# Rolling an 8192 x 8192 matrix by 100 columns: long pieces from column 100 on, and only the wrapped columns through SBUF

## The chip, the cores and the metric

The kernel runs on one core of a Trainium2 chip. The metric is the time of one execution on the device, in microseconds (us). Before the change the median of three runs was 828.28 us (827.91 to 828.41). The core has several engines that issue work: SP and ACT, which here only issue transfers; POOL, which issues transfers through a queue of its own; and DVE, which copies inside SBUF, the core's on-chip memory of 128 partitions. All transfers, whoever issued them, are carried out by 16 DMA engines.

## The reference

```python
def setup_inputs():
    return {"x": np.random.randn(8192, 8192).astype(np.float32), "shift": 100}

def reference(x, shift):
    return np.roll(x, shift, axis=1)
```

Every row is moved 100 columns to the right, and its last 100 columns come round to its beginning: `out[r, 100:] = x[r, :8092]` and `out[r, :100] = x[r, 8092:]`. Nothing is computed; 268.44 MB are read and 268.44 MB are written.

## The kernel before

Each output row is split at a column `a`. With a shift `s = 100`, L20 rounds it up to 128, and L21 and L22 add another 128, so `a = 256`. `g = a - s = 156` is the number of columns between the wrapped part and the split.

**The long pieces** (L36 to L43) are columns 256 to 8191 of the output. They are copied from memory to memory without passing SBUF. A block is 64 rows; the view takes its rows as 16 x 4, and for each of the four values of `j` one transfer moves 16 rows of 7936 columns (31,744 bytes a row, 496 KB a transfer). SP issues those of even `j`, ACT those of odd `j`. There are 128 blocks. In the last four, each transfer is cut into two halves at a column `mid`, so that the last transfers are smaller. SP and ACT thus issue 264 transfers each. In bytes of a row, a long piece is read from byte 624 (column 156) and written from byte 1024 (column 256).

**The edge pieces** (L60 to L80) are columns 0 to 255 of the output. They go through SBUF in 16 stages of 512 rows, four consecutive rows on each of 128 partitions. A stage has a tile `h` that collects the 256 columns of its 512 rows, and a tile `t`.

- L72 loads `t`. In memory the end of a row is followed by the beginning of the next one, so one run of 256 columns holds the last 100 columns of a row and the first 156 of the next row. Each partition loads three such runs, of 1024 bytes.
- L73 loads the last 100 columns of the fourth row (400 bytes) straight into `h`, and L76 the first 156 columns of the first row (624 bytes).
- L74 and L77 are copies on DVE that bring the two parts of the three runs to their places in `h`.
- L80, in a loop of its own after all stages, stores `h`: 512 runs of 1024 bytes, 512 KB, at byte 0 of the output rows.

All loads and stores of the edge pieces are issued by POOL, in the order of the program: three loads for each of 16 stages and then 16 stores. The tiles of all stages fit beside one another (`bufs=n_st`), so no stage waits for a buffer of another. POOL does wait when too many of its transfers are under way, and a store waits for the copies of its stage. The output columns of the two kinds of pieces don't overlap, so neither waits for the other.

Of the kernel before, what the change touches and what calls it, by code (L numbers as in the profile page):

```python
# [1 line left out]

# [4 lines left out]


@with_exitstack
def kernel(  # L10
    ctx: ExitStack,
    tc: tile.TileContext,
    x: bass.AP,
    shift: int,
    out: bass.AP,
):
    nc = tc.nc
    n_rows, n_cols = x.shape
    s = shift % n_cols
    a = -(-s // 128) * 128  # L20
    if 0 < a <= 384 and a + 128 <= n_cols:  # L21
        a += 128  # L22
    g = a - s
    P = nc.NUM_PARTITIONS
    engines = [nc.sync, nc.scalar]
    n_chunks = 16
    rows = n_rows // n_chunks

    xm = x.rearrange("(c e j) w -> c j e w", e=16, j=4)
    om = out.rearrange("(c e j) w -> c j e w", e=16, j=4)
    if a < n_cols:  # L36
        blocks = n_rows // 64
        mid = (a + n_cols) // 256 * 128
        for c in range(blocks):
            parts = ((a, mid), (mid, n_cols)) if c >= blocks - 4 and a < mid else ((a, n_cols),)  # L40
            for j in range(4):
                for lo, hi in parts:
                    engines[j % 2].dma_start(out=om[c, j, :, lo:hi], in_=xm[c, j, :, lo - s:hi - s])  # L43
    if a == 0:
        return


    if a > 512:
        for i in range(n_chunks):
            r = slice(i * rows, (i + 1) * rows)  # L50
            nc.gpsimd.dma_start(out=out[r, :s], in_=x[r, n_cols - s:])
            if g > 0:
                nc.gpsimd.dma_start(out=out[r, s:a], in_=x[r, :g])
        return

    Q = 4  # L60
    n_st = n_rows // (P * Q)
    reads = ctx.enter_context(tc.tile_pool(name="reads", bufs=n_st))
    heads = ctx.enter_context(tc.tile_pool(name="heads", bufs=n_st))
    xt = x.rearrange("(k p q) c -> k p q c", q=Q, p=P)
    ot = out.rearrange("(k p q) c -> k p q c", q=Q, p=P)
    tiles = []
    for k in range(n_st):
        t = reads.tile([P, Q - 1, a], x.dtype)
        h = heads.tile([P, Q, a], x.dtype)
        lead = bass.AP(tensor=x.tensor, offset=(k * P * Q + 1) * n_cols - s,  # L70
                       ap=[[Q * n_cols, P], [n_cols, Q - 1], [1, a]])
        nc.gpsimd.dma_start(out=t[:], in_=lead)  # L72
        nc.gpsimd.dma_start(out=h[:, Q - 1, :s], in_=xt[k, :, Q - 1, n_cols - s:])  # L73
        nc.vector.tensor_copy(h[:, :Q - 1, :s], t[:, :, :s])  # L74
        if g > 0:
            nc.gpsimd.dma_start(out=h[:, 0, s:], in_=xt[k, :, 0, :g])  # L76
            nc.vector.tensor_copy(h[:, 1:, s:], t[:, :, s:])  # L77
        tiles.append(h)
    for k, h in enumerate(tiles):
        nc.gpsimd.dma_start(out=ot[k, :, :, :a], in_=h[:])  # L80


# [1 line left out]
_INS = ['x', 'shift']  # L84
_OUTS = [((8192, 8192), 'float32')]

_NUMBERS = {'shift': 100}


# [26 lines left out]
```

## Time and profile before

| | |
|---|---|
| Median of three runs | 828.28 us (827.91 to 828.41) |
| Span of the profiled execution | 828.0 us |
| Long pieces, SP's and ACT's queues | 2 x 130.04 MB |
| Edge pieces, POOL's queue | 16.78 MB |
| Mean rate of the DMA engines | 334 GB/s |
| Memory traffic, read and written | 648 GB/s |
| Busy: DVE, POOL | 12.3 us, 41.3 us |
| Landing of a long transfer after its issue, median | 12.7 us |
| Landing of an edge store after its issue, median | 108.2 us |

The profiled execution is known by its span alone, from the first to the last instruction, 828.0 us, which is 0.3 us from the median of the runs. The profile's rate of the DMA engines counts a moved byte once. Its memory traffic counts a byte of a long piece twice, since it is read from memory and written to memory, and a byte of an edge piece once in its load and once in its store, since the other end of each is in SBUF. Queue rows give packets, megabytes and the share of the 16 engines' time that the packets took; an engine is occupied while it waits for memory too. In the views of the profile, q1 and q10 are the queues of SP and ACT, q0 is POOL's.

### The profile page before, as it was taken

The page shows a single profiled execution, that of the slowest core. Times are in us where ns is not written, and L with a number is a line of the kernel's source. Part 1 is how long each engine was busy: PE and PEld are TensorE (multiplying, and loading weights), DVE is VectorE, ACT ScalarE, POOL GpSimd, SP SyncE. Part 2 cuts the span into 40 slices and gives each one's busy share as a digit, 9 for nine tenths or more (in the row PEclk, how much of TensorE's full clock was granted, in tenths as well). Part 3 has the DMA queues.
Part 4 walks back from the last instruction along what each step waited for, and adds up shares of the span by engine and source line. Part 5 has one row for each costly group of instructions (what it writes and reads, how often), then busy time and mean ns, then how long its engine had stood idle before and what let it go on. Part 6 is the DMA issues. An engine that isn't in the chain of part 4 may idle for free. (4 is left out here: it accounts for less than half of the span.)

```text
span 828.0 us, 689 instructions
## 1 busy us (share of the span) xinstructions
DVE 12.3 (1%) x32; POOL 41.3 (5%) x68
## 2 busy tenths in 40 slices
DVE  0000000000010000000000000000000000000000
POOL 2011000000021100000000000000000000000000
DMA  9999999999999999999999999999999999999998
GB/s 308 340 350 334 344 340 337 337 339 344 337 342 348 352 351 345 354 339 346 347 341 344 333 325 325 319 330 333 330 324 322 335 330 328 322 331 328 327 314 300
DMA packets 22278, 276.90 MB, mean 334 GB/s; under 512 B 9473, under 2 KB 9729, under 8 KB 13825
## 3 DMA queue, kind: packets, MB, share of 16 engines
q1 hardware_dynamic: 8448, 130.04, 46.1%
q10 hardware_dynamic: 8448, 130.04, 44.7%
q0 software_dynamic: 5376, 16.78, 8.4%
q14 instruction: 6, 0.04, 0.0%
HBM read 268.44 MB, written 268.44 MB: 648 GB/s over the span
## 5 line engine op out<-in xcount | busy, mean ns | idle before, releaser
L80 POOL DMA_DIRECT2D out_dram<-h x16 | 11.5, 724 | 126.6 <-DMA out_dram<-h 86.8
L76 POOL DMA_DIRECT2D h<-in_x_dram x16 | 8.7, 542 | 141.4 <-DMA t<-in_x_dram 141.4
L72 POOL DMA_DIRECT2D t<-in_x_dram x16 | 12.2, 762 | 30.8 <-DMA h<-in_x_dram 30.0
L73 POOL DMA_DIRECT2D h<-in_x_dram x16 | 8.9, 559 | 39.9 <-DMA h<-in_x_dram 39.9
L74 DVE COPY h<-t 128x300 f32<-128x300 f32 x16 | 6.1, 382 | 260.2 <-DMA t<-in_x_dram 260.2
L77 DVE COPY h<-t 128x468 f32<-128x468 f32 x16 | 7.5, 467 | 0.0
L97 POOL MEMSET const-float32-0.0<- 128x1 f32 x1 | 0.1, 99 | 0.2 <-issue 0.2
L97 POOL MEMSET const-bfloat16-1.0<- 128x1 bf16 x1 | 0.1, 102 | 0.0
L97 POOL MEMSET const-float32-1.0<- 128x1 f32 x1 | 0.1, 99 | 0.0
L97 POOL MEMSET const-uint8-127<- 128x1 uint8 x1 | 0.1, 99 | 0.0
## 6 DMA issues: line engine op xcount, KB each, us to landing
out_dram<-in_x_dram ACTq DMA_DIRECT2D x248, 496.0 KB, 12.7
out_dram<-in_x_dram SPq DMA_DIRECT2D x248, 496.0 KB, 12.7
out_dram<-h POOLq DMA_DIRECT2D x16, 512.0 KB, 108.2
t<-in_x_dram POOLq DMA_DIRECT2D x16, 384.0 KB, 50.6
out_dram<-in_x_dram SPq DMA_DIRECT2D x16, 248.0 KB, 6.0
out_dram<-in_x_dram ACTq DMA_DIRECT2D x16, 248.0 KB, 5.9
h<-in_x_dram POOLq DMA_DIRECT2D x16, 78.0 KB, 43.2
h<-in_x_dram POOLq DMA_DIRECT2D x16, 50.0 KB, 49.9
```

What stands on the lines that cost most here:

```text
L72: nc.gpsimd.dma_start(out=t[:], in_=lead)
L73: nc.gpsimd.dma_start(out=h[:, Q - 1, :s], in_=xt[k, :, Q - 1, n_cols - s:])
L74: nc.vector.tensor_copy(h[:, :Q - 1, :s], t[:, :, :s])
L76: nc.gpsimd.dma_start(out=h[:, 0, s:], in_=xt[k, :, 0, :g])
L77: nc.vector.tensor_copy(h[:, 1:, s:], t[:, :, s:])
L80: nc.gpsimd.dma_start(out=ot[k, :, :, :a], in_=h[:])
L97: nc = _bacc.Bacc("TRN2", target_bir_lowering=False, num_devices=1)
```

## The change

`a` becomes the shift itself, 100, so `g` is 0. The long pieces are now columns 100 to 8191: 8092 columns, 32,368 bytes a row, read from byte 0 of a row and written from byte 400. `mid` becomes 4096, so the halves in the last four blocks have 3996 and 4096 columns instead of 3968 each. Of the edge pieces only the 100 wrapped columns are left. A stage has one tile, one load of 512 runs of 400 bytes and one store of the same runs at byte 0 of the output rows. The tile `t`, the loads of L72, L73 and L76 and the copies on DVE are gone.

```diff
     s = shift % n_cols
-    a = -(-s // 128) * 128
-    if 0 < a <= 384 and a + 128 <= n_cols:
-        a += 128
+    a = s
     g = a - s
...
     Q = 4
     n_st = n_rows // (P * Q)
-    reads = ctx.enter_context(tc.tile_pool(name="reads", bufs=n_st))
-    heads = ctx.enter_context(tc.tile_pool(name="heads", bufs=n_st))
+    ends = ctx.enter_context(tc.tile_pool(name="ends", bufs=n_st))
...
     for k in range(n_st):
-        t = reads.tile([P, Q - 1, a], x.dtype)
-        h = heads.tile([P, Q, a], x.dtype)
-        lead = bass.AP(tensor=x.tensor, offset=(k * P * Q + 1) * n_cols - s,
-                       ap=[[Q * n_cols, P], [n_cols, Q - 1], [1, a]])
-        nc.gpsimd.dma_start(out=t[:], in_=lead)
-        nc.gpsimd.dma_start(out=h[:, Q - 1, :s], in_=xt[k, :, Q - 1, n_cols - s:])
-        nc.vector.tensor_copy(h[:, :Q - 1, :s], t[:, :, :s])
-        if g > 0:
-            nc.gpsimd.dma_start(out=h[:, 0, s:], in_=xt[k, :, 0, :g])
-            nc.vector.tensor_copy(h[:, 1:, s:], t[:, :, s:])
+        h = ends.tile([P, Q, s], x.dtype)
+        nc.gpsimd.dma_start(out=h[:], in_=xt[k, :, :, n_cols - s:])
         tiles.append(h)
     for k, h in enumerate(tiles):
-        nc.gpsimd.dma_start(out=ot[k, :, :, :a], in_=h[:])
+        nc.gpsimd.dma_start(out=ot[k, :, :, :s], in_=h[:])
```

## The prediction

> **What bounds the kernel now.** I read first the page's shares, queues and memory totals, then the waits, then the transfer view cut into three stretches of time. The order matters: the first view shows that only transfers count, the last shows which side of the transfers is full.
>
> ```profile
> span 828.0 us, 689 instructions
> DVE 12.3 (1%) x32; POOL 41.3 (5%) x68
> DMA  9999999999999999999999999999999999999998
> ...
> q1 hardware_dynamic: 8448, 130.04, 46.1%
> q10 hardware_dynamic: 8448, 130.04, 44.7%
> q0 software_dynamic: 5376, 16.78, 8.4%
> ...
> HBM read 268.44 MB, written 268.44 MB: 648 GB/s over the span
> ```
>
> Compute is 1% and 5%. The 16 transfer engines are occupied from the first slice to the last: 46.1 + 44.7 + 8.4 = 99.2%. q1 and q10 carry the long pieces that SP and ACT issue, q0 the edge pieces that POOL issues. The issuing engines wait for transfers:
>
> ```profile
> SPq L43 <- DMA out_dram<-in_x_dram: 680.3, 260, 4.9
> DVE h L74 <- DMA t<-in_x_dram: 260.2, 16, 22.7
> POOL h L76 <- DMA t<-in_x_dram: 141.4, 13, 14.6
> ```
>
> POOL issues its last store at 379.6 us of 828.0 (the source view of L80: "241.2 to 379.1" and "242.2 to 379.6"), SP and ACT their last pieces at 820.3 and 822.4, so the long pieces end the run.
>
> An occupied transfer engine may still be waiting for memory. Three stretches tell: only q0 loads run beside the long pieces from 0 to 240 us, nearly only q0 stores from 240 to 470 us, almost nothing from 480 to 780 us. The transfer view of each, in this order:
>
> ```profile
> DMA packets 7352, 80.96 MB, mean 337 GB/s; under 512 B 2975, under 2 KB 3194, under 8 KB 5039
> q10 hardware_dynamic: 2293, 36.54, 41.5%
> q1 hardware_dynamic: 2319, 36.86, 40.2%
> q0 software_dynamic: 2738, 7.55, 17.2%
> ...
> DMA packets 7014, 79.63 MB, mean 346 GB/s; under 512 B 2555, under 2 KB 2592, under 8 KB 4788
> q1 hardware_dynamic: 2228, 35.56, 46.1%
> q10 hardware_dynamic: 2212, 35.05, 42.6%
> q0 software_dynamic: 2572, 9.00, 12.0%
> ...
> DMA packets 6203, 98.14 MB, mean 327 GB/s; under 512 B 3092, under 2 KB 3092, under 8 KB 3113
> q1 hardware_dynamic: 3085, 48.96, 50.5%
> q10 hardware_dynamic: 3089, 49.08, 48.7%
> q0 software_dynamic: 27, 0.09, 0.1%
> ```
>
> A long piece goes from memory to memory and counts twice there; a q0 byte counts once, its other end is SBUF. Memory traffic is then (2 x 73.40 + 7.55) / 240 = 643 GB/s, (2 x 70.61 + 9.00) / 230 = 653 GB/s and (2 x 98.04 + 0.09) / 300 = 654 GB/s. The engines' own rate varies by 6% (327 to 346 GB/s), the memory's by 1.7%, and part of that is the start. So I read memory traffic, at about 654 GB/s, as the limit. The total, 2 x 260.05 + 16.78 = 536.87 MB, takes 821.0 us at 653.9 GB/s; the other 7.0 us of the span are start, tail and the slower load stretch.
>
> **The change, part by part.** The sum is made against the profiled span, 828.0 us; the median of the runs is 828.28, 0.3 us more.
>
> *Bytes.* The long pieces grow from 7936 to 8092 columns: 260.05 to 265.16 MB, 5.11 more, each counted twice. q0 shrinks from 256 columns to 100, loaded and stored: 16.78 to 6.55 MB. Memory traffic: 2 x 265.16 + 6.55 = 536.87 MB, the same as before, and so 821.0 us again. Cost 0. Everything that follows is about how well these bytes are moved.
>
> *Fewer short transfers.* The load stretch ran at 643 instead of 654 GB/s: 240 x (1 - 643.1 / 653.9) = 4.0 us. The first slice of the page ran at 308 GB/s against 340 in the next one: 20.7 x (1 - 308 / 340) = 1.9 us of it are the start. The remaining 2.1 us are the loads'. They fall from 8.39 to 3.28 MB, so I take -1.3 us (between -2.1 and 0).
>
> *POOL, DVE.* 48 loads of about 0.54 to 0.76 us each become 16, the 16 stores stay, 32 copies (12.3 us) go. The waits of L74 (260.2 us) and L76 (141.4 us) go with them. Nothing of this touches SP, ACT or their queues, and the end of POOL's work was at 380 us; cost 0, covered by 400 us of long pieces. The wait that is late next is that of each store for its one load; behind it on POOL are only further stores, for which nobody waits but the end. q0 would have to become some four times slower for POOL to end the run.
>
> *Long pieces' issues.* Still 264 each on SP and ACT, in the same order. The halves of the last four blocks are 3996 and 4096 columns instead of 3968 twice. A half landed in 5.9 us (248 KB), so the larger takes 5.9 x 256 / 248 = 6.1: +0.2 us at the tail (0 to 0.2).
>
> *The seam inside each output row.* This is what the trace doesn't show. Before, every write to the output began at byte 0 or 1024 of a row, or half-way; the reads of the long pieces began at byte 624. After, the reads begin at byte 0 and the writes at byte 400, and the head of the row ends there. In each of 8192 rows two writers meet at byte 400, inside one block of the memory if blocks are larger than 16 bytes. Bounds: the lower is a gain. If an odd beginning costs the same on a read as on a write, it moves from one side to the other and the cost is 0; if only reads pay, it is a saving of the size I take below, 11.4 us. For the size I use the price of one short transfer on q0. There were 16 x (384 + 128 + 128) loads and 16 x 512 stores of pieces, 18,432 in all. They took 16.78 MB / 653.9 GB/s = 25.7 us of the memory's time, 1.39 ns each of the span; their engine time was 8.4% of 828 = 69.6 us, 3.77 ns each. One extra short access per row therefore costs 8192 x 1.39 ns = 11.4 us as memory time, 30.9 us as engine time. I take 11.4, because the three stretches say that memory binds; the ends are -11.4 and +30.9 us.
>
> "DMA: Bandwidth & Descriptors" of the Trainium skill (Specifications) says that a transfer under 512 B makes the engine read, modify and write; the 400 B stores fall under it, the 1024 B stores did not. By that rule alone the stores' 3.28 MB would be read once more, an estimate of 5.0 us, and the time 832; no row of this case shows such a store, for the 400 B pieces of before were loads.
>
> Sum: 828.0 - 1.3 + 0.2 + 11.4 = 838.3 us; with the 0.3 us between span and median 838.6. I predict 838.5, slower by 1.2%.
>
> **The rivals.**
>
> *Every write suffers, not only the seam.* If a long piece is written in blocks counted from its own beginning, every block of 32 KB rows lies across a block of the memory and is partly written twice. Price: 1% of the writes' 265.16 MB moved again is 2.65 MB / 653.9 = 4.06 us. One block in eight again costs 50.7 us, giving 879 us; every block again would give 828 + 406. For it: with memory full, nothing hides extra traffic. Against it: the reads of every long piece already begin at an odd byte, 624, and the total still holds 654 GB/s, so one side at least manages odd beginnings well. It decides from about 5% extra writes (20 us), where it outweighs the seam.
>
> *Transfer engines bind: faster.* If engine time counts and not memory, q0's price matters: loads 17.2% of 240 us for 7.55 MB = 5.47 us per MB, stores 12.0% of 230 us for 9.00 MB = 3.07. After: 3.28 x (5.47 + 3.07) = 28.0 us instead of 69.6, 41.6 saved; long pieces 5.11 / 260.08 of 90.8% of 828 = 14.8 added. 828 - 41.6 + 14.8 = 801 us. For it: 99.2% occupancy. Against it: the occupancy stays near full at 327 and at 346 GB/s, so it includes waiting. A milder way to the same sign is that only reads pay for odd beginnings: 828 - 11.4 - 1.1 = 815.5. The point from which it is faster: a seam cheaper than 1.1 us.
>
> *Nothing to see.* The seam is absorbed by the memory controller, the byte total is equal, and the time is 827 to 829 us. For it: the equal 536.87 MB. Against it: it needs a seam cost that is both positive and under 3 us.
>
> **How the numbers follow.** Seam cost, about 830 to 850 us: 0.40. Every write suffers, above 850: 0.27. Nothing to see, within 0.2% (about what a measurement of this kernel can tell from no change): 0.13. Faster, 800 to 826: 0.20. So slower 0.67, same 0.13, faster 0.20. The range: about half of the fast case lies below 820, and a little under half of the every-write case above 880; leaving out these 0.2 gives 820 to 880. The likeliest case's own range is 830 to 850.
>
> **What would show it.** Right: memory traffic in a stretch without q0 (after about 250 us) falls a little, from 654 to some 645 GB/s, q0's share falls from 8.4% to 3 or 4%, and the span ends at 835 to 845. If every write suffers, the engines' rate without q0 falls well under 327 GB/s, to 307 at 879 us. If q0's share stays near 8% with only 6.55 MB, the short stores are the cost rather than the seam of the long pieces. If engines bind, the rate without q0 rises. The prediction is wrong most easily in the seam's price, which rests on q0's short transfers and not on any write at an odd byte.

## The result and the profile after

The changed kernel took 839.07 us (median, 836.42 to 842.34) beside 828.18 us before (827.91 to 828.41): 1.0128 times before, 95% interval 1.0106 to 1.0149. That is 10.6 us slower by the ratio, on a forecast of 838.5 us. The size and the sign were right, the size in part by luck. The experiments below show a cost of writes that begin or end at byte 400, which is the kind of cost that the prediction had in mind; but two terms of its sum were off in opposite directions.

The page of the kernel after gives the engines, the queues (packets, MB, share of the 16 engines' time) and the memory's total:

```profile
span 834.6 us, 609 instructions
POOL 23.7 (3%) x36
DMA  9999999999999999999999999999999999999998
...
q1 hardware_dynamic: 8448, 132.60, 48.3%
q10 hardware_dynamic: 8448, 132.60, 47.5%
q0 software_dynamic: 2048, 6.56, 3.6%
...
HBM read 268.44 MB, written 268.44 MB: 643 GB/s over the span
```

DVE has no work left, POOL's queue fell from 8.4% to 3.6%, and the time still grew. The bytes at the memory are the same; the mean rate is 643 instead of 648 GB/s. The issuing engines still wait for transfers. Of the kernel after, first the waits (total us, times, longest), then the source view of its store line L69 (shortest, median and longest ns of one, first and last start in us):

```profile
SPq L41 <- DMA out_dram<-in_x_dram: 687.9, 259, 6.5
POOL h L66 <- DMA h<-in_x_dram: 50.0, 8, 8.2
POOL out_dram L69 <- DMA out_dram<-h: 47.8, 8, 7.8
POOL out_dram L69 <- DMA h<-in_x_dram: 29.1, 6, 6.1
```

```profile
L69 POOL DMA_DIRECT2D out_dram<-h x16: 709/709/817, 68.4 to 151.0; - x16
```

POOL issues its last store at 151.0 us instead of 379.6, so the edge stores run in the first quarter of the span. This makes it easy to see what they cost. Here is the transfer view from 60 to 180 us, first of the kernel before (edge loads beside the long pieces), then of the kernel after (the last edge loads, of which none is issued after 62.6 us, and the edge stores):

```profile
DMA packets 3664, 40.81 MB, mean 340 GB/s; under 512 B 1506, under 2 KB 1610, under 8 KB 2492
q10 hardware_dynamic: 1162, 18.48, 43.4%
q1 hardware_dynamic: 1182, 18.73, 40.3%
q0 software_dynamic: 1320, 3.61, 15.8%
```

```profile
DMA packets 3461, 39.28 MB, mean 327 GB/s; under 512 B 1409, under 2 KB 1409, under 8 KB 2375
q1 hardware_dynamic: 1086, 17.61, 45.8%
q10 hardware_dynamic: 1084, 17.55, 41.8%
q0 software_dynamic: 1291, 4.12, 12.8%
```

Counting long pieces twice, the memory moved (2 x 37.21 + 3.61) / 120 = 650 GB/s before and (2 x 35.16 + 4.12) / 120 = 620 GB/s after. Against the 654 GB/s of the undisturbed stretch, these 120 us lose 0.7 us before and 6.2 us after, 5.5 of the 6.6 us between the two spans. From 480 to 780 us, where only long pieces run, the kernel after shows:

```profile
DMA packets 6057, 98.07 MB, mean 327 GB/s; under 512 B 3026, under 2 KB 3026, under 8 KB 3026
q1 hardware_dynamic: 3026, 48.98, 50.2%
q10 hardware_dynamic: 3029, 49.08, 49.6%
```

2 x 98.06 / 300 = 654 GB/s, the same as before. In this profile most of the cost lies where the edge pieces run, and the long pieces from byte 400 show hardly any (from 240 to 540 us they moved 652 GB/s). That was not where the prediction had looked for it.

Two cautions. The profiled execution after is the fastest of the six (836.42 us). And a run's time exceeds its span by 1.8 us here and by 1.7 or 1.8 in every profiled execution below; the execution profiled before isn't known by its time, and with the same gap it would have been one of about 829.8 us. So spans compare less well than medians, and a small cost spread over the whole span can hide in one profile.

### The profile page after: what moved, and what is told of

Same layout as the page of the kernel before. It is cut to its first block, busy times and chain, and to the rows that moved or that the text cites. A ratio compares the mean times of both kernels' runs of the same rounds, so it can differ in the third digit from the quotient of the medians.

```text
span 834.6 us, 609 instructions
## 1 busy us (share of the span) xinstructions
POOL 23.7 (3%) x36
## 5 line engine op out<-in xcount | busy, mean ns | idle before, releaser
L69 POOL DMA_DIRECT2D out_dram<-h x16 | 11.5, 725 | 76.9 <-DMA out_dram<-h 47.8
L66 POOL DMA_DIRECT2D h<-in_x_dram x16 | 12.1, 758 | 50.9 <-DMA h<-in_x_dram 50.0
```

Of the source, the lines that this page charges most:

```text
L66: nc.gpsimd.dma_start(out=h[:], in_=xt[k, :, :, n_cols - s:])
L69: nc.gpsimd.dma_start(out=ot[k, :, :, :s], in_=h[:])
```

## The experiments

Ratios are to the kernel before, run beside each experiment on the same chip. 1% is 8.3 us. "Odd" is used below for a beginning or an end of a read or a write that is not a multiple of 32 bytes in its row, and "even" for one that is. That 32 is the number is a reading of the runs, in which byte 400 is the only odd place of a write.

**Without the edge stores.** All edge loads stay, 15 of the 16 edge stores go.

```diff
-    for k, h in enumerate(tiles):
-        nc.gpsimd.dma_start(out=ot[k, :, :, :s], in_=h[:])
+    h = tiles[0]
+    nc.gpsimd.dma_start(out=ot[0, :, :, :s], in_=h[:])
```

> The kernel after, but 15 of the 16 edge stores are left out (columns 0 to 99 of most rows are never written); the long pieces still begin at column 100. Left out are 3.07 MB of writes, 4.7 us at 653.9 GB/s. If the long pieces' odd beginning is the cost (the seam of the prediction): 839.1 - 4.7 = 834 us. If the 400 B stores are the cost: 828.2 - 4.7 - 1.1 = 822 us, and the memory rate from 60 to 200 us is back at about 650 GB/s from the 617 seen after. The spread of the runs (836 to 842 after) goes away with whichever part causes it.

Measured: 826.26 us beside 827.27, ratio 0.9987 (0.9973 to 1.0000). It lies between the two expectations, so neither the stores nor the long pieces' beginning is the whole. Against the kernel after, 1.28 + 0.13 = 1.41% or 11.7 us went, 7.0 more than the 4.7 us of the bytes left out, give or take 2.1. The time stayed 4 us above the 822 us that were expected if the stores were all of the cost. The rate from 60 to 200 us rose to (2 x 43.96 + 1.44) / 140 = 638 GB/s, not to 650; in the kernel after it is 627 there (the 617 of the expectation is about that kernel's mean from 0 to 160 us). Part of what is missing is a hole from 95 to 110 us, in which the engines moved only 289 GB/s; what caused it isn't known.

**The edge stores of before, split.** The long pieces stay aligned and all bytes stay; only the edge stores are cut in two, at column 100, 104, 128 or 144. The diff for 100:

```diff
-        nc.gpsimd.dma_start(out=ot[k, :, :, :a], in_=h[:])
+        nc.gpsimd.dma_start(out=ot[k, :, :, :100], in_=h[:, :, :100])
+        nc.gpsimd.dma_start(out=ot[k, :, :, 100:a], in_=h[:, :, 100:])
```

At column 100:

> The kernel before, with its aligned long pieces; each edge store is split at column 100 into one of 400 B runs and one of 624 B runs, the same bytes in all. If stores under 512 B are read and written again: 828.2 + 5.0 (8192 x 400 B at 653.9 GB/s) to + 6.4 (8192 x 512 B) = 833 to 835 us. If only the long pieces' odd beginning costs: 828.2 us. If each further short run costs 1.39 ns: 828.2 + 11.4 = 839.6 us.

At column 128:

> The kernel before; each edge store is split at column 128 into two of 512 B runs. If stores under 512 B are the cost: 828.2 us, no change, since none is shorter than 512 B. If the number of short runs is the cost: 828.2 + 11.4 = 839.6 us. If only the long pieces' beginning matters: 828.2 us.

At column 144:

> The kernel before; each edge store is split at column 144 into runs of 576 B (from byte 0) and of 448 B (from byte 576, a multiple of 64). The split at column 100 cost 8.9 us. If a store under 512 B is read and written again, whatever its beginning: 448 x 8192 / 653.9 = 5.6 us, 833 us. If only a beginning or an end that is no multiple of 64 costs: no change, 827.3 us. If any end within a 512 B block costs as at column 100: 836 us.

At column 104:

> The kernel before; each edge store is split at column 104, into runs of 416 B (a multiple of 32, not of 64) and 608 B. The split at byte 400 cost 8.9 us, those at 512 and 576 nothing. If blocks of 64 B or more count: +8.9 us, 836 us. If blocks of 32 B count: no change, 827 us.

| Split at | Runs, bytes | Ratio to before (95% interval) |
|---|---|---|
| column 100 | 400 + 624 | 1.0108 (1.0090 to 1.0127) |
| column 104 | 416 + 608 | 0.9992 (0.9982 to 1.0003) |
| column 128 | 512 + 512 | 1.0003 (0.9991 to 1.0015) |
| column 144 | 576 + 448 | 0.9994 (0.9985 to 1.0003) |

This table narrows the cost down. Twice as many short stores cost nothing (128). Stores of 416 and 448 bytes cost nothing (104, 144), so it isn't a matter of being shorter than 512 bytes. Four columns decide between 0 and 8.9 us: 400 is no multiple of 32, 416 is one, 13 x 32, and no multiple of 64. Two things stay open. Byte 400 is the only odd place that was tried. And in every run of this document, a write with one odd edge also has a length that is no multiple of 32 (400, 624 or 32,368 bytes, say), and a store with one begins or ends at an odd place of SBUF too. So the runs show which writes cost, but not whether the place in memory or the length is the reason; a write of 416 bytes from an odd byte on would tell. The transfer views from 240 to 540 us, while the stores run, of the splits at columns 100, 104 and 128, in this order:

```profile
q1 hardware_dynamic: 2880, 45.69, 47.0%
q10 hardware_dynamic: 2872, 45.56, 42.8%
q0 software_dynamic: 2888, 9.19, 10.7%
```

```profile
q1 hardware_dynamic: 2952, 46.92, 45.8%
q10 hardware_dynamic: 2941, 46.76, 44.6%
q0 software_dynamic: 3210, 9.42, 10.0%
```

```profile
q1 hardware_dynamic: 2966, 47.11, 46.5%
q10 hardware_dynamic: 2963, 47.02, 45.9%
q0 software_dynamic: 2750, 8.83, 7.9%
```

The memory moved (2 x 91.25 + 9.19) / 300 = 639 GB/s beside the stores cut at column 100, against (2 x 93.68 + 9.42) / 300 = 656 and (2 x 94.13 + 8.83) / 300 = 657. The share of q0 is no measure of the cost: it is 10.7% at column 100, but 10.0% at column 104, which cost no time.

**Edge stores of 400 or of 416 bytes, long pieces aligned.** In both, the long pieces begin at column 128, byte 512, so no other write meets the end of the edge stores, and the two kernels differ by four columns of width. With the width the beginning of the edge loads changes too, from byte 32,368 of a row, which is odd, to byte 32,352, which is even.

```diff
+    a = 128
     if a < n_cols:
```

and for 416 bytes in addition

```diff
-        h = ends.tile([P, Q, s], x.dtype)
-        nc.gpsimd.dma_start(out=h[:], in_=xt[k, :, :, n_cols - s:])
+        h = ends.tile([P, Q, s + 4], x.dtype)
+        nc.gpsimd.dma_start(out=h[:], in_=xt[k, :, :, n_cols - s - 4:])
...
-        nc.gpsimd.dma_start(out=ot[k, :, :, :s], in_=h[:])
+        nc.gpsimd.dma_start(out=ot[k, :, :, :s + 4], in_=h[:])
```

400 bytes:

> The kernel after, but the long pieces begin at column 128, byte 512 (columns 100 to 127 are never written), so they are aligned and share no block with the 400 B edge stores. 2 x 0.92 MB less, 2.8 us. If the 400 B stores are the cost by themselves: 839.1 - 2.8 = 836 us, or at least 828.2 - 2.8 - 1.1 + 5.0 = 829 us if only their bytes are read again. If the long pieces' odd beginning, or two writers in one block, is the cost: 828.2 - 2.8 - 1.1 = 824 us.

416 bytes:

> As the kernel with 400 B edge stores and long pieces from column 128, but the edge loads and stores are 104 columns wide, 416 B, a multiple of 32 (columns 0 to 103 get the last 104 columns of the row, columns 104 to 127 are left out). That kernel took 1.0024 times before. 2 x 0.13 MB more, 0.4 us. If the odd end of a 400 B store costs by itself, without another writer in its block, some 4.5 us go: 0.997 to 0.998 of before, about 825 beside 827.3. If the shortness of the stores costs, or two writers in one block: 1.003 of before.

Measured: 1.0024 (1.0013 to 1.0035) with 400 bytes, 829.16 us beside 827.27; 0.9984 (0.9967 to 1.0001) with 416 bytes, 825.85 us beside 826.42. The difference is 0.40%, 3.3 us; with 0.4 us for the additional bytes, the 400-byte pieces cost 3.7 us more than the even ones, give or take 1.7. It is put down to the odd end of the stores, since odd reads of the long pieces show no such cost below; the loads' odd beginning wasn't tried by itself. The cost needs no second write at the same byte. The 829 us that were expected if the stores' bytes are read again were met with 400 bytes, but the stores of 416 bytes, which are under 512 too, didn't pay this. The views from 60 to 180 us agree, 400 bytes first: (2 x 35.84 + 3.48) / 120 = 626 GB/s, then (2 x 36.52 + 4.30) / 120 = 645.

```profile
q1 hardware_dynamic: 1120, 18.19, 46.6%
q10 hardware_dynamic: 1099, 17.65, 42.6%
q0 software_dynamic: 1098, 3.48, 11.4%
```

```profile
q1 hardware_dynamic: 1128, 18.16, 44.4%
q10 hardware_dynamic: 1133, 18.36, 42.3%
q0 software_dynamic: 1626, 4.30, 12.4%
```

**The long pieces by themselves.** Only the first edge stage is left (`for k in range(1)`), and the long pieces begin at column 100, or at 128 (`a = 128` as above), or at 128 with the source read from column 0:

```diff
-                    engines[j % 2].dma_start(out=om[c, j, :, lo:hi], in_=xm[c, j, :, lo - s:hi - s])
+                    engines[j % 2].dma_start(out=om[c, j, :, lo:hi], in_=xm[c, j, :, lo - 128:hi - 128])
```

From column 100 (writes begin at byte 400, odd; reads begin at byte 0, even, and end at byte 32,368, odd):

> The kernel after with only the first of its 16 edge stages (the other rows' columns 0 to 99 are never written): the long pieces from column 100 by themselves. Memory traffic 2 x 265.16 + 0.41 = 530.7 MB, 811.6 us at 653.9 GB/s, and about 6.3 us of start and tail: 818 us if the odd beginning of the long pieces costs nothing, 828 us or more if it has the size that the prediction gave it (11.4 us). Against the next kernel the difference is 2.8 us from the bytes alone.

From column 128 (writes even; reads begin at byte 112 and end at byte 32,368, both odd):

> As the kernel before this one, but the long pieces begin at column 128 (columns 100 to 127 are never written), on a multiple of 512 B. 2 x 264.24 + 0.41 = 528.9 MB, 808.8 + 6.3 = 815 us by every theory; the kernel from column 100 lies 2.8 us above it if its odd beginning is free, and up to 14 us above it if the seam costs 11.4 us.

From column 128, read from column 0 (both even):

> As the kernel with only the long pieces from column 128, but they are read from column 0 instead of column 28 (the rows are moved by 128 columns, not by 100, and columns 0 to 127 are left out but for one stage), so that neither reads nor writes begin at an odd byte; the bytes are the same. That kernel took 811.7 us beside 826.9 before. If an odd beginning costs a read as much as a write (3.5 us): 808.2 us. If only writes pay: 811.7 us.

Measured: 818.00 us beside 826.91 (0.9897, 0.9884 to 0.9910); 811.67 us beside 826.91 (0.9815, 0.9803 to 0.9828); 812.73 us beside 829.28 (0.9801, 0.9788 to 0.9815). The second was expected at 815 us by every theory and took 3 us less: start and tail were put too high, so the first, at the 818 us that were expected of a free beginning, wasn't free either. The difference of the two counts. On the same chip it is 6.3 us by the medians, of which 2.8 are bytes: the odd beginning of the long pieces' writes costs 3.5 us (4.0 by the ratios), give or take 1.5. Even reads in the third are worth 0.14%, 1.2 us with an uncertainty of 1.5, so a cost of odd reads isn't shown. The views of the three from 240 to 540 us, in this order:

```profile
q10 hardware_dynamic: 3042, 49.27, 50.5%
q1 hardware_dynamic: 3038, 49.08, 49.0%
```

```profile
q1 hardware_dynamic: 3058, 49.33, 50.5%
q10 hardware_dynamic: 3060, 49.39, 49.2%
```

```profile
q10 hardware_dynamic: 3055, 49.33, 50.2%
q1 hardware_dynamic: 3053, 49.23, 49.5%
```

98.35, 98.72 and 98.56 MB: the odd writes moved 0.4% less than the second kernel in the same time, and 0.2% less than the third. Over 812 us, 0.4% is 3 us. So thin a cost is hardly seen in single profiles: from 480 to 780 us, with nothing beside the long pieces, the four profiles with odd ones moved 650 to 654 GB/s and the six with even ones 654 to 656. The times show it.

**The kernel after once more.**

> The kernel after, unchanged, beside the others on the same chip: 1.28% above before, as measured, 837 to 839 us. By the parts measured so far: 400 B stores 5 to 6 us, the rest of the 10.9 us from the odd beginning of the long pieces or from the 400 B loads. The profile should again lose its time between 60 and 200 us if the edge pieces are the cause, and evenly over the span if the long pieces are.

Measured: 837.11 us beside 826.91, 1.0123 (1.0102 to 1.0145). Its profile again drops from 60 to 180 us, to (2 x 35.81 + 3.64) / 120 = 627 GB/s, and this time runs at 2 x 97.50 / 300 = 650 GB/s from 480 to 780 us, so a loss shows in both places. The two views:

```profile
q1 hardware_dynamic: 1108, 17.97, 45.4%
q10 hardware_dynamic: 1104, 17.84, 42.4%
q0 software_dynamic: 1141, 3.64, 12.5%
```

```profile
q1 hardware_dynamic: 3014, 48.78, 50.1%
q10 hardware_dynamic: 3012, 48.72, 49.3%
```

**The split at column 112.** This version writes all of the output and was meant to beat both kernels: byte 448 is even, and the edge pieces are less than half of those before.

```diff
-    a = -(-s // 128) * 128
-    if 0 < a <= 384 and a + 128 <= n_cols:
-        a += 128
+    a = -(-s // 16) * 16
```

> The kernel before with the split of each row at column 112 (byte 448, the next multiple of 64 above 400) instead of 256: all outputs are written, the edge pieces carry 7.34 instead of 16.78 MB, with loads of 448, 400 and 48 B. If writes that begin and end on multiples of 64 are free however short, and the edge loads' excess (about 3 us in before) falls with their bytes: 825.5 us. If an edge store under 512 B costs: 833 us. If the number of short loads counts and not their bytes: 827 us.

Measured: 1.0006 (0.9994 to 1.0018), no difference from before, so the gain to 825.5 us didn't come. Shifting the split from column 256 to 112 keeps all of the time, as long as the split is even. It gains nothing, so the kernel before stays as good as any that was found.

## Why the prediction was right, and where it was not

*Memory binds.* Borne out. With the same 536.87 MB at the memory, the q0 share fell by more than half and the time did not fall. The rival in which the transfer engines bind, with 801 us, is excluded. For the base of the sum: the long pieces alone from column 128 took 811.67 us for 528.90 MB, 808.8 us at 653.9 GB/s, so 2.8 us lie outside the bytes.

*Fewer short transfers, -1.3 us.* This term did not come. Before, the excess over bytes and base is 826.91 - 821.0 - 2.8 = 3.1 us, and it holds all edge loads and stores. In the kernel with 416-byte edge pieces and aligned long pieces it is 0.9984 x 826.9 - 535.30 / 0.6539 - 2.8 = 4.1 us, give or take 1.4, with 41% of before's edge bytes and no odd write. So the excess did not fall with the bytes. The kernel that keeps all loads and one of the 16 stores still has 0.9987 x 826.9 - 533.80 / 0.6539 - 2.8 = 6.7 us. With 3.5 us for the odd writes of the long pieces, 3.2 are left, which seem to go with the loads. Their number of runs hardly changed, from 10,240 to 8192; whether it is the number was not tested.

*POOL, DVE, 0 us.* Right: POOL issued its last store at 151 us, and what it waits for is waited for by nobody else.

*The halves at the tail, +0.2 us.* As forecast, the halves landed in 6.1 to 6.3 us instead of 5.9 or 6.0. From the last issue to the end of the span it was 6.7 us instead of 5.6, in one profile of each.

*The seam, +11.4 us.* The kind held: the writes that begin or end at byte 400 cost, and the same seam cut into the edge stores of the kernel before, with nothing else changed, cost 8.9 us. The price did not come from where it was derived. The prediction took 1.39 ns for one short access per row; but this is just the memory's time for the 910 bytes that an edge transfer carried on average (16.78 MB / 18,432), not what an access costs beside its bytes. A further access is free here: 8192 more stores changed nothing when they were cut at byte 416, 512 or 576. What costs is the odd write: 3.7 us for the edge stores and 3.5 us for the long pieces, over 8192 rows 0.45 and 0.43 ns each; the split at column 100, with two odd edges in a row, gives 0.54 ns for each. So the seam is worth 7.2 us by its parts and 8.9 us by the split, 4.2 or 2.5 less than the 11.4 of the prediction. That the total came within 0.6 us of the forecast is partly luck: the 1.3 us to be gained did not come, and some 2 us belong to no measured part.

The sum of measured parts is 821.0 + 2.8 + 4.1 + 3.7 + 3.5 = 835.1 us, against 837.1 measured beside these runs. The rest of 2 us is within the uncertainty of the parts. Whether two odd writes that meet cost more than each alone is left open: by the ratios, the kernel with only odd stores plus the difference of the two kernels with long pieces alone makes 1.0024 + 0.9897 - 0.9815 = 1.0106, and the kernel after measured 1.0123 on the chip of the last two, 1.4 us more with an uncertainty of 2.5.

*Where to look for it.* The prediction expected the rate without q0 to fall to some 645 GB/s. It stood at 654 and 650 in the two profiles after. Half of the odd edges belong to the edge stores, and their cost is paid while they run, at 620 and 627 GB/s. The q0 share of 3.6% came as foreseen; the span of 834.6 us lies just under the 835 to 845.

*The rule on short stores.* By "DMA: Bandwidth & Descriptors" of the Trainium skill (Specifications), a transfer under 512 B is read, modified and written. The prediction's estimate of 832 us from this had the right sign and less than half of the size. In this case no store of 416 or 448 bytes that began and ended on a multiple of 32 took measurable time; the measurement decides, and it says that a length under 512 B is not what cost.

*The other rivals.* That every block of an odd write suffers, with 879 us, falls with the long pieces' 3.5 us, 0.9% of their writes' traffic by the prediction's own 4.06 us for 1%. (By that price it would have outweighed the seam's 11.4 us from 2.8% on, not from 5%.) That only reads pay is excluded in the other direction: of the two kernels with long pieces alone, the one whose reads begin even and whose writes begin odd was the slower.

## What to carry to other kernels

When memory binds and the bytes stay the same, look at the edges of the writes: here an edge at byte 400 of a row cost some 0.45 to 0.54 ns, one at byte 416 nothing measurable, and these four columns decided over 1%. Splitting, shortening or lengthening the stores did nothing as long as the edges were multiples of 32 bytes. Put the split between two writers on such a byte, even if some bytes must then go a longer way; rounding further gained nothing here. A cost that is spread thinly over the whole span is found by a pair of runs, not in one profile.

## What the runs showed of the hardware

- Edge stores of 1024 bytes cut into 416 + 608 or 576 + 448 bytes took the time of uncut ones (0.9992 and 0.9994 of before), those cut into 400 + 624 did not (1.0108).
- Of the edges tried, the odd multiple of 16 (byte 400) costs and the odd multiple of 32 (byte 416) does not; a multiple of 64 is not needed. Whether the place in memory or the length of the run decides was not separated.
- Odd reads showed no cost beyond 1.2 us with an uncertainty of 1.5 for 8192 rows that begin and end odd, while the odd beginning of the writes showed 3.5.
- The memory moved 649 to 658 GB/s, read and written, on the one core in the long stretches with nothing beside the long pieces; 639 beside odd edge stores cut from before's, 620 to 627 beside the edge pieces of the kernel after.
